# One fused hybrid layer on one core: left-over column tiles in another order, and three due times moved

## The chip, the cores and the metric

The kernel runs on one core of one Trainium2 chip. The core has five engines that run side by side, each working through its own queue in a fixed order: PE (matrix products), DVE (vector), ACT (scalar functions), POOL (a second, general elementwise engine) and SP (which here issues the DMAs). The metric is the device time of one execution in microseconds (us); lower is better.

## The reference

A layer with three branches over 2048 tokens of width 1024:

```python
h = rms_norm(x, pre_norm_g);  z = h @ w_in                      # 29 column tiles of 128
out_a = spatial_gating(u_a, v_a, ...) * silu(g_a)               # branch a
out_b = conv_module(val_b, glu_b, ...) * silu(g_b)              # branch b: 31-tap causal convolution,
                                                                # layer norm, silu, 256x256 product
out_c = rwkv7_mix(z_c, ...) * silu(g_c)                         # branch c: recurrence over tokens
mix = concat(out_a, out_b, out_c) @ w_out
x = x + rms_norm(mix, post_norm_g)
return x + (p @ ple_w) * sigmoid(x @ ple_gate_w + ple_gate_b)
```

In `rwkv7_mix` every output row also gets a bonus, `sum(r*k*r_k) * v` per head.

## The kernel before, in words

The first product, `h @ w_in`, is done in float32 as three products of a high and a low part, 48 matmuls of 128x512 per column tile and half of the tokens (line 300; two tiles at line 312 are transposed). There are two halves of 1024 tokens. In each, PE goes through the 29 column tiles in the order of the table `ORDER`; `TG[ct]` is the place of tile `ct` in it. Tiles 10 and 11 are branch b's gates, 25 to 28 those of branch c. The last six places of the second half are left over (`NT = 6`): they are not done in the column loop but, matmul by matmul, as filler among the recurrence of branch c, by the generator `tail`. Its first 45 matmuls are put ahead of the recurrence by `go(9.75)`.

All work up to the recurrence is written as generators that yield a due time in units of column tiles; `at` turns a due time into a priority, and a scheduler lays every engine's queue out from the priorities and its own time estimate of each instruction. So queues are fixed when the program is built, and an engine never overtakes an instruction that waits. From the recurrence on, PE's and DVE's orders are those of the code, but work of an earlier due time may still be laid between.

The steps that matter here:

- `s_pw` normalises the convolution's output: `parts` splits a tile into a high part (ACT, line 231) and a low part (DVE, line 232), `sums` adds over partitions on PE (line 240); mean (line 625), squares (630), square roots (637, ACT), reciprocals in four pieces (`recip`, line 245, DVE), product and silu (641, 642). Half 0 then does both gates of branch b: `pw_in` is the silu of the gate (653), `pw_out` the 256x256 product (661, PE, four matmuls a gate into two banks) and its product with the gate (664, DVE). In half 1 `tail` calls `pw_in` and `pw_out`.
- `s_prep`, last lines: the bonus of a head pair `p`: product (546), `parts`, `sums` (552, which calls line 240), product with v (553), bias (554), store (555).
- `norm_h(2)` and `norm_h(3)` load the second half's tokens. Their scale is transposed by PE (218) into two banks named `c` and copied by ACT (219). `build_h` then multiplies eight tiles by it (line 268), for one group of 512 tokens on DVE and for the other on POOL.
- `scores` (820, 825, 829) and `inverse` (861 to 886) prepare the recurrence; line 603 is branch a's spatial product.

Matmuls write to banks: the pools `m` and `c` have two each (`mps`), `z` two. The tile pool `pg` has one buffer, and every gate passes through it.

Of the kernel before, what the change touches and what calls it, by code (L numbers as in the profile page):

```python
# [34 lines left out]
def hybrid_kernel(ctx, tc, x, x_t, w_in, vecs, wup, pw_w, sgu_wt, sgu_lnb, sgu_b,  # L35
# [23 lines left out]
    def new(tag, shape=(128, 1024), dt=F32):  # L59
        return sb.tile(list(shape), dt, tag=tag, bufs=BUFS[tag], name=nm(tag))  # L60

    def at(v):

        tc.cur_priority = int(v * 1000)
# [17 lines left out]
    def mps(shape=(128, 512), tag="m"):  # L82
        return psp.tile(list(shape), F32, tag=tag, bufs=2, name=nm(tag))
# [58 lines left out]
    def col(i):  # L142
        return vc[:, i:i + 1]
# [84 lines left out]
    def parts(src, eng):  # L228

        hl = [new("mk", dt=F32R) for _ in range(2)]  # L230
        nc.scalar.copy(hl[0], src)
        eng.tensor_tensor(out=hl[1], in0=src, in1=hl[0], op=ALU.subtract)
        return hl

    def sums(ps, ones, hls, sl):

        n = 0
        for hl in hls:
            for t in hl:
                nc.tensor.matmul(ps, lhsT=ones, rhs=t[:, sl], start=(n == 0), stop=(n == 2 * len(hls) - 1))  # L240
                n += 1

    def recip(t):
        for g in range(4):
            nc.vector.reciprocal(t[:, g * 256:(g + 1) * 256], t[:, g * 256:(g + 1) * 256])  # L245
# [100 lines left out]

    ORDER = [2, 8, 3, 6, 24, 9, 7, 12, 16, 13, 20, 17, 21, 4, 14, 0, 18, 22, 15, 19, 5, 23, 1, 10, 11, 25, 26, 27, 28]
    NG = len(ORDER)  # L350
    NT = 6
    LORD = [2, 3] + [ct for ct in ORDER if ct not in (2, 3)]
    TG = {ct: i for i, ct in enumerate(ORDER)}
    W, Z, H, X = {}, {}, {}, {}
# [38 lines left out]
    def s_gemm():  # L393
        for half in range(2):
# [5 lines left out]
            while n < (NG if half == 0 else NG - NT):  # L400
                two = half == 0 and n == NG - 2
                yield b0 + n
                cts = ORDER[n:n + 2] if two else ORDER[n:n + 1]
                for ct in cts:
# [50 lines left out]
    def s_prep(half, p, st):  # L455

        b0 = half * NG
# [91 lines left out]
        for g in range(2):  # L549
            sp = mps()  # L550
            sl = slice(g * 512, (g + 1) * 512)
            sums(sp, ones64, [hl], sl)
            nc.vector.tensor_tensor(out=vs_[:, sl], in0=sp, in1=vs_[:, sl], op=ALU.mult)
        nc.scalar.activation(vs_, vs_, AF.Identity, bias=col(V_LB + p))
# [58 lines left out]
    def s_pw(half, st):  # L613

        b0 = half * NG
        t0 = half * HT
        yield b0 + NG - 8.5
        cv = [st["cv", ct] for ct in range(2)]
        hls = [parts(c, nc.vector) for c in cv]
        for g in range(2):  # L620
            sl = slice(g * 512, (g + 1) * 512)
            mp = mps()
            sums(mp, onesm, hls, sl)
            for ct in range(2):
                nc.vector.tensor_tensor(out=cv[ct][:, sl], in0=cv[ct][:, sl], in1=mp, op=ALU.subtract)
        yield b0 + NG - 7.6
        hls = []
        for ct in range(2):
            sq = new("mk")
            nc.scalar.activation(sq, cv[ct], AF.Square)  # L630
            hls.append(parts(sq, nc.vector))
        rb = new("mk")
        for g in range(2):
            sl = slice(g * 512, (g + 1) * 512)
            vp = mps()
            sums(vp, onesm, hls, sl)
            nc.scalar.activation(rb[:, sl], vp, AF.Sqrt, bias=epsr[:, 1:2])  # L637
        yield b0 + NG - 7.0
        recip(rb)
        for ct in range(2):  # L640
            nc.vector.tensor_tensor(out=cv[ct], in0=cv[ct], in1=rb, op=ALU.mult)
            nc.scalar.activation(cv[ct], cv[ct], AF.Silu, scale=col(V_CG + ct), bias=col(V_CBB + ct))
        if half == 0:
            for ct in range(2):
                yield b0 + TG[10 + ct] + 0.1
                at(b0 + TG[10 + ct] - 5)
                pw_in(half, ct, st)
                for _ in pw_out(half, ct, st):
                    pass

    def pw_in(half, ct, st):
        st["gb", ct] = gb = new("pg")
        nc.scalar.activation(gb, Z[half, 10 + ct], AF.Silu)

    def pw_out(half, ct, st):
        gb = st["gb", ct]
        for g in range(2):
            sl = slice(g * 512, (g + 1) * 512)
            pp = mps(tag="c" if half == 0 else "m")
            for k in range(2):  # L660
                nc.tensor.matmul(pp, lhsT=pw_t[:, k, ct * 128:(ct + 1) * 128], rhs=st["cv", k][:, sl],
                                 start=(k == 0), stop=(k == 1))
            yield 1.72
            nc.vector.scalar_tensor_tensor(out=gb[:, sl], in0=pp, scalar=col(V_PB + ct), in1=gb[:, sl],
                                           op0=ALU.add, op1=ALU.mult)
        nc.sync.dma_start(out=ab_s[2 + ct, :, half * HT:half * HT + HT], in_=gb)
# [3 lines left out]
    for half in range(2):  # L670
        st = {}
        S += [s_lora(half, st), s_conv(half, 0, st), s_conv(half, 1, st)]
        S += [s_prep(half, p, st) for p in range(4)]
        S += [s_sgu(half, st), s_pw(half, st)]
# [12 lines left out]
    def tail():  # L687

        cts = ORDER[NG - NT:]
        for n, ct in enumerate(cts[:-2]):  # L690
# [661 lines left out]
```

## Time and profile before

| | |
|---|---|
| time, median of 3 runs | 1438.82 us (1437.01 to 1440.38) |
| profiled execution: its time, its span | 1437.73 us, 1436.0 us |
| PE busy | 1378.8 us, 96% of the span |
| DVE, ACT, POOL busy | 1009.2, 568.6, 246.0 us |
| mean granted clock of PE | 0.987 of full speed |

The profile is of one execution. A row of a timeline gives the start and the length of a run of equal instructions on one engine, and in brackets how long the engine stood idle before it and what ended that. The granted clock of PE is given as a share of 2.4 GHz; 0.50 is 1.2 GHz. Lines in the rows are those of the kernel before. PE's columns of half 0 end at 394.5 us, and the recurrence's first scores run at 701.5.

### The profile page before, as it was taken

The numbers are of one execution on the slowest core, as the hardware profiler recorded it, in microseconds if no ns is written. First come the engines' busy times: TensorE is split into PE (matmuls) and PEld (weight loads), VectorE is DVE, ScalarE is ACT, GpSimd is POOL, SyncE is SP. The second block draws the span as 40 slices with busy tenths as digits, with TensorE's granted clock in tenths as the row PEclk, the third lists the DMA queues.
The fourth block names the chain that finished last, engine by engine and source line by source line (L and its number), as shares of the span: only waits on it lengthen the run. The fifth ranks groups of instructions, "written<-read, shape, count | busy, mean of one in ns | idle before, by whom it ended". The sixth has DMA issues, their size and how long they took to land.

```text
span 1436.0 us, 24389 instructions
## 1 busy us (share of the span) xinstructions
PE 1378.8 (96%) x9701; PEld 1102.1 (77%) x9701; DVE 1009.2 (70%) x2003; ACT 568.6 (40%) x897; POOL 246.0 (17%) x284
## 2 busy tenths in 40 slices
PE   7999999999999999999898999999998999999998
PEld 6876877887898778778676777777776777888887
DVE  6599994885537999777667588678779544545453
ACT  6334444555332343453433443544543543111121
POOL 5442221221501000000111211211221101111120
PEclk9999999999999999999899899999999999999999
DMA  8432465679534558855723833242331534242331
GB/s 335 148 147 88 150 212 181 191 277 286 208 116 153 175 175 241 231 153 192 227 89 121 291 113 95 76 140 82 109 100 56 169 124 153 99 139 99 118 117 44
DMA packets 158311, 223.29 MB, mean 155 GB/s; under 512 B 58236, under 2 KB 108149, under 8 KB 158198
## 3 DMA queue, kind: packets, MB, share of 16 engines
q1 hardware_dynamic: 158066, 221.68, 46.9%
q8 instruction: 76, 1.25, 0.4%
q14 instruction: 37, 0.30, 0.1%
q10 hardware_dynamic: 132, 0.06, 0.0%
HBM read 132.58 MB, written 89.13 MB: 154 GB/s over the span
## 4 chain that ended last, share of the span: by engine, by line
PE 73%; DVE 20%; ACT 3%; issue 2%; DMA 1%; DVEq 0%; ACTq 0%
PE z L300 33%; PE z L1164 12%; PE z L1051 8%; DVE inv L452 5%; PE c L1141 3%; PE z L312 3%; DVE inv L873 3%; PE m L820 3%; DVE inv L878 2%; PE m L240 1%; DVE mk L245 1%; DVE inv L861 1%; PE m L1120 1%; DVE L L976 1%; DMA w<-in_gate_w_dram 1%
## 5 line engine op out<-in xcount | busy, mean ns | idle before, releaser
L300 PE MATMUL z<-h,w 128*128 128x512 f32 x2592 | 630.5, 398 | 0.0
L300 PEld LDWEIGHTS z<-h,w 128*128 128x128 f32 x2592 | 484.0, 189 | 118.0 <-issue 6.4
L1051 PE MATMUL z<-h,w 128*128 128x512 f32 x768 | 206.0, 412 | 0.7 <-DVE w L1038 0.7
L452 DVE SCALAR_TENSOR_TENSOR inv<-inv,vc,inv 128x1024 f32<-128x1024 f32 x120 | 173.0, 1460 | 1.4
L1051 PEld LDWEIGHTS z<-h,w 128*128 128x128 f32 x768 | 139.9, 192 | 31.7 <-DVE w L1038 1.1
L283 POOL TENSOR_TENSOR w<-w,w 128x1024 fp32r<-128x1024 f32 x26 | 74.3, 2857 | 235.9 <-PE z L300 178.1
L1164 PE MATMUL z<-L,w 128*128 128x512 f32 (+1 forms) x384 | 96.3, 394 | 0.0
L1164 PE MATMUL z<-h,w 128*128 128x512 f32 (+1 forms) x384 | 93.1, 390 | 0.8 <-DVE inv L1147 0.8
L1148 ACT ACTIVATE inv<-inv 128x512 f32<-128x512 f32 (+1 forms) x33 | 20.4, 620 | 181.7 <-DVE inv L1147 181.7
L873 DVE TENSOR_TENSOR inv<-inv,inv 128x48 f32<-128x48 f32 (+23 forms) x464 | 85.8, 219 | 2.3
L878 DVE TENSOR_TENSOR inv<-inv,inv 128x48 f32<-128x48 f32 (+23 forms) x464 | 84.3, 217 | 1.2
L1164 PEld LDWEIGHTS z<-h,w 128*128 128x128 f32 x384 | 71.3, 188 | 17.4 <-DVE inv L1147 1.2
L1147 DVE TENSOR_TENSOR inv<-z,L 128x512 f32<-128x512 f32 (+1 forms) x32 | 21.9, 683 | 87.8 <-PE z L1164 87.8
L1164 PEld LDWEIGHTS z<-L,w 128*128 128x128 f32 x384 | 70.4, 188 | 15.3
L1108 POOL TENSOR_TENSOR inv<-inv,pg 128x1024 f32<-128x1024 f32 x16 | 38.3, 2394 | 216.9 <-DMA inv<-mx_s 117.6
L245 DVE RECIPROCAL mk<-mk 128x256 f32<-128x256 f32 x40 | 65.8, 1708 | 12.1 <-ACT mk L637 8.0
L825 DVE TENSOR_TENSOR mk<-m,mask 128x512 f32<-128x512 f32 x58 | 37.6, 685 | 35.9 <-PE m L820 31.4
L978 POOL TENSOR_TENSOR ri<-ri,pc 128x256 f32<-128x256 f32 x31 | 19.5, 630 | 236.8 <-DVE L L976 226.6
L829 ACT COPY inv<-mk 32x128 f32<-32x128 f32 x128 | 37.8, 295 | 52.9 <-DVE mk L825 50.1
L820 PE MATMUL m<-L,L 64*128 64x128 f32 x464 | 44.5, 299 | 10.1 <-DVE yn L1002 8.6
L312 PE MATMUL z<-w,h 128*128 128x256 f32 x384 | 52.6, 293 | 0.9 <-ACT h L262 0.9
L312 PEld LDWEIGHTS z<-w,h 128*128 128x128 f32 x384 | 50.3, 197 | 3.1 <-ACT h L262 1.6
(244 smaller groups left out, 1932.9 us busy)
## 6 DMA issues: line engine op xcount, KB each, us to landing
w_s<-w SPq DMA_DIRECT2D x58, 512.0 KB, 3.3
w<-w_s SPq DMA_DIRECT2D x58, 512.0 KB, 5.4
w<-in_w_in_dram SPq DMA_DIRECT2D x26, 512.0 KB, 3.5
L<-in_x_dram SPq DMA_DIRECT2D x16, 512.0 KB, 7.3
ar_s<-L SPq DMA_DIRECT2D x16, 512.0 KB, 5.0
wo_s<-w SPq DMA_DIRECT2D x16, 512.0 KB, 4.2
L<-ar_s SPq DMA_DIRECT2D x32, 256.0 KB, 3.1
L<-bk_s SPq DMA_DIRECT2D x32, 256.0 KB, 4.1
```

The lines of the kernel that those rows point to most:

```text
L245: nc.vector.reciprocal(t[:, g * 256:(g + 1) * 256], t[:, g * 256:(g + 1) * 256])
L283: nc.gpsimd.tensor_tensor(out=ws[1], in0=wr, in1=ws[0], op=ALU.subtract)
L300: nc.tensor.matmul(z[:, g * 512:(g + 1) * 512], lhsT=ws[a][:, k * 128:(k + 1) * 128], rhs=h[:, b, k, :], start=(n == 0), stop=(n == 23))
L312: nc.tensor.matmul(z[:, i * 256:(i + 1) * 256], lhsT=h[:, b, k, i * 128:(i + 1) * 128], rhs=ws[k // 4][a][:, (k % 4) * 256:(k % 4 + 1) * 2 ...
L452: nc.vector.scalar_tensor_tensor(out=ac, in0=y[:, i:i + HT], scalar=col(V_CW + 2 * i + ct), in1=ac, op0=ALU.mult, op1=ALU.add)
L820: nc.tensor.matmul(sp[par][:, p, :], lhsT=bk[lo:lo + 64, p, :], rhs=ar[lo:lo + 64, p, :], start=True, stop=True)
L873: nc.vector.tensor_tensor(out=tmp[:, o:o + n, :m], in0=tl[:, lo:hi, m:m + 1].to_broadcast([128, n, m]), in1=ml[:, m, :m].unsqueeze(1).to_b ...
L878: nc.vector.tensor_tensor(out=tl[:, lo:hi, :m], in0=tl[:, lo:hi, :m], in1=tmp[:, o:o + n, :m], op=ALU.add)
L1051: nc.tensor.matmul(mx[:, nh * 512:(nh + 1) * 512], lhsT=oT[a][:, k, :], rhs=wo[k // 4][:, b, k % 4, nh * 512:(nh + 1) * 512], start=(k == ...
L1108: nc.gpsimd.tensor_tensor(out=x2, in0=x2, in1=pg[0], op=ALU.mult)
L1141: nc.tensor.matmul(pp, lhsT=pT[:, a, k, :], rhs=gw[8 + k][b][:, nh * 512:(nh + 1) * 512], start=(n == 0), stop=(n == 5))
L1164: nc.tensor.matmul(z, lhsT=xT[a][:, k, :], rhs=gw[k][b][:, sl], start=(k == 0 and n == 0), stop=(k == 7 and n == 2))
```

## The change

Five places are edited. In `ORDER`, tiles 25 and 26 now stand ahead of 10 and 11 (places 23 and 24 instead of 25 and 26). The table serves both halves, so in half 0 the gates of branch b are the places 25 and 26 of the column loop, and in half 1 they are the third and fourth of the left-over tiles. In half 1 the three due times of the convolution's norm are 1, 1 and 0.95 tiles later. And the bonus sums of the last head pair in half 1 get the priority of 2*NG - NT + 0.1 = 52.1, behind the start of the recurrence's part at 52 (they had 51.5).

```diff
-    ORDER = [..., 5, 23, 1, 10, 11, 25, 26, 27, 28]
+    ORDER = [..., 5, 23, 1, 25, 26, 10, 11, 27, 28]
...
             sl = slice(g * 512, (g + 1) * 512)
+            if half == 1 and p == 3:
+                at(2 * NG - NT + 0.1)
             sums(sp, ones64, [hl], sl)
...
-        yield b0 + NG - 8.5
+        yield b0 + NG - (8.5 if half == 0 else 7.5)
...
-        yield b0 + NG - 7.6
+        yield b0 + NG - (7.6 if half == 0 else 6.6)
...
-        yield b0 + NG - 7.0
+        yield b0 + NG - (7.0 if half == 0 else 6.05)
```

From line 552 on, lines of the changed kernel are two higher. In the orders below a bank or buffer carries its own number, so c_2625 and c_2693 are tiles that use the two `c` banks one after the other.

PE at the end of half 0, before. Here z_2590 is tile 25, c_2441 and c_2445 are the 256x256 product for branch b's first gate (tile 10), c_2509 and c_2513 for its second (tile 11), m_2368 and m_2378 branch a's product.

```order
L661 MATMUL c_2441<-inv_699,jk_121 128x512
L661 MATMUL c_2445<-inv_699,jk_121 128x512
L300 MATMUL z_2590<-h_224,w_2347 128x512
L661 MATMUL c_2441<-inv_894,jk_121 128x512
L661 MATMUL c_2445<-inv_894,jk_121 128x512
L300 MATMUL z_2590<-h_224,w_2346 128x512 x2
L603 MATMUL m_2368<-yc_124,mk_130 64x128 x8
L603 MATMUL m_2378<-yc_124,mk_131 64x128 x3
L661 MATMUL c_2509<-inv_699,jk_121 128x512
L661 MATMUL c_2509<-inv_894,jk_121 128x512
```

The same place of the program, now: z_2574 is tile 10, z_2642 tile 11, z_2706 tile 27, w_2444 and w_2445 tile 11's weights (high and low part), c_2625 and c_2629 the first gate's product, c_2693 and c_2697 the second's.

```order
L300 MATMUL z_2574<-h_289,w_2347 128x512
L663 MATMUL c_2625<-inv_699,jk_121 128x512
L663 MATMUL c_2625<-inv_894,jk_121 128x512
L663 MATMUL c_2629<-inv_699,jk_121 128x512
L663 MATMUL c_2629<-inv_894,jk_121 128x512
L300 MATMUL z_2642<-h_224,w_2444 128x512 x2
L663 MATMUL c_2693<-inv_699,jk_121 128x512
L663 MATMUL c_2693<-inv_894,jk_121 128x512
L663 MATMUL c_2697<-inv_699,jk_121 128x512
L663 MATMUL c_2697<-inv_894,jk_121 128x512
L300 MATMUL z_2706<-h_224,w_2504 128x512 x2
L300 MATMUL z_2642<-h_224,w_2445 128x512
```

Behind the bonus sums of half 0's last pair stood 11 column matmuls (L300), then the first product; now 57 column matmuls, branch a's product and the transposes of line 218 stand between. The two gates' products are now two column matmuls apart.

DVE at the end of half 0, before: the products with the gates (pg), branch a's (mk_2367), the copies for the transposed scale (L215) and the eight multiplications of the next half's tokens (L268).

```order
L664 SCALAR_TENSOR_TENSOR pg_2439<-c_2441,vc,pg_2439 128x512
L664 SCALAR_TENSOR_TENSOR pg_2439<-c_2445,vc,pg_2439 128x512
L607 SCALAR_TENSOR_TENSOR mk_2367<-m_2368,vc,yn_125 128x512
L215 COPY mk_2542<-rs_2539 128x512
L215 COPY mk_2574<-rs_2571 128x512
L607 SCALAR_TENSOR_TENSOR mk_2367<-m_2378,vc,yn_125 128x512
L610 TENSOR_TENSOR mk_2367<-mk_2367,mk_2136 128x1024
L664 SCALAR_TENSOR_TENSOR pg_2507<-c_2509,vc,pg_2507 128x512
L664 SCALAR_TENSOR_TENSOR pg_2507<-c_2513,vc,pg_2507 128x512
L268 TENSOR_TENSOR L_2550<-L_2550,mk_2542 128x512 x2
```

And now, from the first of the eight on:

```order
L268 TENSOR_TENSOR L_2534<-L_2534,mk_2526 128x512 x2
L268 TENSOR_TENSOR L_2536<-L_2536,mk_2526 128x512 x2
L268 TENSOR_TENSOR L_2538<-L_2538,mk_2526 128x512 x2
L268 TENSOR_TENSOR L_2540<-L_2540,mk_2526 128x512 x2
L666 SCALAR_TENSOR_TENSOR pg_2623<-c_2625,vc,pg_2623 128x512
L666 SCALAR_TENSOR_TENSOR pg_2623<-c_2629,vc,pg_2623 128x512
L666 SCALAR_TENSOR_TENSOR pg_2691<-c_2693,vc,pg_2691 128x512
L666 SCALAR_TENSOR_TENSOR pg_2691<-c_2697,vc,pg_2691 128x512
```

All four products with the gates, which are what reads the `c` banks, went from ahead of the eight multiplications to behind them.

DVE ahead of the recurrence, before: reciprocals of the norm (mk_4740), the low part for the bonus sums (mk_4849), the norm's products (L641), the bonus products (L553, which read the banks m_4852 and m_4856), branch a's.

```order
L245 RECIPROCAL mk_4740<-mk_4740 128x256 x4
L232 TENSOR_TENSOR mk_4849<-L_4473,mk_4848 128x1024
L641 TENSOR_TENSOR inv_3223<-inv_3223,mk_4740 128x1024
L641 TENSOR_TENSOR inv_3421<-inv_3421,mk_4740 128x1024
L553 TENSOR_TENSOR L_4724<-m_4852,L_4724 128x512
L553 TENSOR_TENSOR L_4724<-m_4856,L_4724 128x512
L607 SCALAR_TENSOR_TENSOR mk_4862<-m_4863,vc,yn_125 128x512
```

And now:

```order
L245 RECIPROCAL mk_4826<-mk_4826 128x256 x2
L232 TENSOR_TENSOR mk_4841<-L_4473,mk_4840 128x1024
L245 RECIPROCAL mk_4826<-mk_4826 128x256 x2
L555 TENSOR_TENSOR L_4702<-m_4844,L_4702 128x512
L555 TENSOR_TENSOR L_4702<-m_4848,L_4702 128x512
L643 TENSOR_TENSOR inv_3223<-inv_3223,mk_4826 128x1024
L643 TENSOR_TENSOR inv_3421<-inv_3421,mk_4826 128x1024
L609 SCALAR_TENSOR_TENSOR mk_4854<-m_4855,vc,yn_125 128x512
```

The low part now stands between the two halves of the reciprocals, and the bonus products ahead of the norm's. On PE the four bonus sums follow, now as before, on all eight sums of squares, but those end later:

```order
L300 MATMUL z_4922<-h_2839,w_4649 128x512
L240 MATMUL m_4827<-mk_4817,onesm 128x512
L240 MATMUL m_4833<-mk_4817,onesm 128x512
L240 MATMUL m_4827<-mk_4822,onesm 128x512
L240 MATMUL m_4833<-mk_4822,onesm 128x512
L240 MATMUL m_4827<-mk_4823,onesm 128x512
L240 MATMUL m_4833<-mk_4823,onesm 128x512
L240 MATMUL m_4844<-mk_4840,ones_83 128x512
L240 MATMUL m_4848<-mk_4840,ones_83 128x512
L240 MATMUL m_4844<-mk_4841,ones_83 128x512
L240 MATMUL m_4848<-mk_4841,ones_83 128x512
L605 MATMUL m_4855<-yc_124,mk_133 64x128 x8
```

Before, the last sums of squares (m_4741, m_4747) had 11 column matmuls of the first left-over tile (z_4922) and eight transposes between themselves and the bonus sums; now those stand ahead of the last sums of squares.

## Rows read from the trace of the kernel before

**Rows 1.** The page: busy time of all engines, and the chain that ended last by engine.

```profile
PE 1378.8 (96%) x9701; PEld 1102.1 (77%) x9701; DVE 1009.2 (70%) x2003; ACT 568.6 (40%) x897; POOL 246.0 (17%) x284
...
PE 73%; DVE 20%; ACT 3%; issue 2%; DMA 1%; DVEq 0%; ACTq 0%
```

**Rows 2.** What PE itself waited for over the whole span: engine, tile, line, the engine and line waited for, us in total, times, longest.

```profile
PE m L240 <- ACT mk L231: 5.5, 3, 3.4
...
PE m L240 <- DVE mk L232: 3.5, 2, 2.6
...
PE m L603 <- DVE L L553: 1.6, 1, 1.6
```

**Rows 3.** Timeline of PE at the end of half 0: start, length, line, what, how many.

```profile
337.05 2.73 PE L300 MATMUL z<-h,w 128*128 128x512 f32 x11
...
345.30 1.99 PE L661 MATMUL c<-inv,jk 128*128 128x512 f32 x4
347.21 0.65 PE L603 MATMUL m<-yc,mk 128*64 128x128 f32 x6
...
350.07 12.59 PE L300 MATMUL z<-h,w 128*128 128x512 f32 x53
362.50 1.04 PE L218 MATMUL c<-ident,mk 128*128 128x128 f32 x8
363.29 31.39 PE L300 MATMUL z<-h,w 128*128 128x512 f32 x134
394.52 11.68 PE L312 MATMUL z<-w,h 128*128 128x256 f32 x96
```

**Rows 4.** The chain that ended last, in order of time: start, length; branch a's product where nothing is laid between it.

```profile
603.20 1.90 PE m L603 x32
```

**Rows 5.** Timeline of DVE at the end of half 0.

```profile
342.63 1.61 DVE L664 SCALAR_TENSOR_TENSOR pg<-c,vc,pg 128x512 f32<-128x512 f32 x2 [0.27 <-PE c L661]
...
363.76 13.08 DVE L268 TENSOR_TENSOR L<-L,mk 128x512 f32<-128x512 f32 x8 [7.14 <-ACT mk L219]
```

**Rows 6.** Timeline of POOL there.

```profile
361.99 2.39 POOL L283 TENSOR_TENSOR w<-w,w 128x1024 fp32r<-128x1024 f32 x1 [9.32 <-ACT w L282]
364.33 13.65 POOL L268 TENSOR_TENSOR L<-L,mk 128x512 f32<-128x512 f32 x8
```

**Rows 7.** Timeline of DVE later, while POOL is idle: one multiplication of two tiles in SBUF, of the size of line 268's.

```profile
665.37 0.69 DVE L517 TENSOR_TENSOR L<-L,L 128x512 f32<-128x512 f32 x1
```

**Rows 8.** PE after a gap of 3.38 us, and stretches of 3 us around it: start and end, length, busy (matmuls), granted clock, DMA share, GB/s.

```profile
141.34 1.22 PE L240 MATMUL m<-mk,ones 128*128 128x512 f32 x2 [3.38 <-ACT mk L231]
...
138.00:141.00 3.00, 0.00 (x0) 0.93 0.00 0
141.00:144.00 3.00, 2.66 (x5) 0.50 0.00 0
144.00:147.00 3.00, 3.00 (x8) 0.50 0.00 0
147.00:150.00 3.00, 3.00 (x13) 0.93 0.53 175
```

**Rows 9.** Timeline of PE ahead of the recurrence.

```profile
686.20 0.61 PE L240 MATMUL m<-mk,onesm 128*128 128x512 f32 x2
...
689.22 1.03 PE L537 MATMUL m<-ident,L 128*128 128x128 f32 x8
691.43 0.98 PE L240 MATMUL m<-mk,ones 128*128 128x512 f32 x2 [1.18 <-ACT mk L231]
695.07 1.22 PE L240 MATMUL m<-mk,ones 128*128 128x512 f32 x2 [2.65 <-DVE mk L232]
697.93 3.68 PE L603 MATMUL m<-yc,mk 128*64 128x128 f32 x32 [1.64 <-DVE L L553]
701.54 0.58 PE L820 MATMUL m<-L,L 64*128 64x128 f32 x1
...
728.69 1.98 PE L661 MATMUL m<-inv,jk 128*128 128x512 f32 x4 [0.67 <-ACT L L839]
```

**Rows 10.** PE in stretches of 1.5 us there (columns as in rows 8).

```profile
693.00:694.50 1.50, 0.00 (x0) 0.68 0.87 285
...
702.00:703.50 1.50, 1.50 (x16) 0.50 0.24 96
703.50:705.00 1.50, 1.50 (x6) 0.91 0.03 8
```

**Rows 11.** Timelines of DVE and ACT there.

```profile
687.35 6.59 DVE L245 RECIPROCAL mk<-mk 128x256 f32<-128x256 f32 x4 [6.14 <-ACT mk L637]
693.85 1.16 DVE L232 TENSOR_TENSOR mk<-L,mk 128x1024 fp32r<-128x1024 f32 x1
694.93 2.35 DVE L641 TENSOR_TENSOR inv<-inv,mk 128x1024 f32<-128x1024 f32 x2
697.19 1.28 DVE L553 TENSOR_TENSOR L<-m,L 128x512 f32<-128x512 f32 x2
...
730.71 0.75 DVE L664 SCALAR_TENSOR_TENSOR pg<-m,vc,pg 128x512 f32<-128x512 f32 x1 [1.12 <-PE m L661]
...
686.62 1.27 ACT L637 ACTIVATE mk<-m,epsr 128x512 f32<-128x512 f32 x2 [9.08 <-PE m L240]
690.33 1.05 ACT L231 CAST mk<-L 128x1024 fp32r<-128x1024 f32 x1
```

More of the change, by code (lines that the diff above doesn't have):

```diff
@@ L345, in split @@
         nc.vector.tensor_tensor(out=dst_lo, in0=src, in1=dst_hi, op=ALU.subtract)
-    ORDER = [2, 8, 3, 6, 24, 9, 7, 12, 16, 13, 20, 17, 21, 4, 14, 0, 18, 22, 15, 19, 5, 23, 1, 10, 11, 25, 26, 27, 28]
+    ORDER = [2, 8, 3, 6, 24, 9, 7, 12, 16, 13, 20, 17, 21, 4, 14, 0, 18, 22, 15, 19, 5, 23, 1, 25, 26, 10, 11, 27, 28]
     NG = len(ORDER)
```

## The prediction

> **What bounds the kernel now.** I read the page's busy shares and its chain first, then what PE waited for, then PE's timeline where the two orders of instructions differ. PE is busy 96% of the span and carries 73% of the chain [rows 1], so a change that moves work without adding any can move the end only by making or removing time in which PE stands, or runs at the low one of its two clock levels. The list of PE's waits is short; the part that this change aims at is the wait for the sums of line 240 and for branch a's product [rows 2]. On the timeline these are the gaps of 1.18, 2.65 and 1.64 us between 690.2 and 697.9 [rows 9], 5.47 us together. The clock makes them dearer: it falls during them and reads 0.50 until shortly after 703.5 [rows 10]. PE never stands between 337 and 394 us, where each run of matmuls begins when the one before ends [rows 3].
>
> PE's order is the same in both kernels up to the last bonus sums of half 0, then differs until the end of half 0's columns, and again from the convolution's norm in half 1 on. I work out both places against the profiled execution, whose own time, 1437.73 us, is 1.09 under the median shown.
>
> **The end of half 0: a new wait.** The four products with the gates on DVE (line 664) now stand behind the eight multiplications of line 268. They free the two c banks, and PE's product for the second gate needs both again, two column matmuls after the first gate's. So I time both sides.
>
> PE: from 337.05 on it has, up to the second gate's product, 57 + 2 column matmuls, branch a's product, eight transposes and the first gate's product. A column matmul takes (362.50 - 350.07)/53 = 0.2345 us, branch a's product 1.90 [rows 4], the transposes 363.29 - 362.50 = 0.79, two L661 rows (four records) 347.21 - 345.30 = 1.91 [rows 3], and there are two such pairs; the second overlaps the column matmuls behind it, so 3.4 to 3.8 for both. That is 337.05 + 13.8 + 1.9 + 0.8 + 3.6 = 357.2.
>
> DVE: 41 of the column matmuls and branch a's product come before the transposes, which so begin at 337.05 + 9.6 + 1.9 = 348.6. Before, the multiplications began 1.26 us after the transposes did (363.76 against 362.50 [rows 3, 5]), so now at 349.8. They take 13.08 us for eight [rows 5], since POOL does the other group's eight at the same time in 13.65 [rows 6]: 1.64 each, against 0.69 for a like multiplication with POOL idle [rows 7]. In the new order the pair still begins together, as both wait for ACT's copies of the same transposes. So they end at 362.9, and the first product with a gate, half of 1.61 [rows 5], at 363.7.
>
> The row shows a multiplication of two SBUF tiles stretched to 2.4 times its length beside POOL. The Trainium skill, SBUF — State Buffer, section "Who interferes with whom", says that a DVE instruction with two SBUF inputs and a GpSimd instruction that reads SBUF take turns at one shared port, the second blocked for the whole of the first; by that the eight and eight alternate, which these rows bear out (13.08 and 13.65 for both together), and nothing about the change lets them run side by side. It is the rule that speaks against the change: without it the eight would end at 349.8 + 8 x 0.69 = 355.3, ahead of PE.
>
> PE therefore stands from 357.2 to 363.7, 6.5 us. What is behind: everything, since nothing on PE's queue can pass the product. After this gap the clock has to be paid too. The nearest row is the gap of 3.38 us at 141: the clock falls during it, reads 0.50 from 141 to 147 and 0.93 in the three us after [rows 8], so PE ran 6.1 us at half its level and lost 3.0. A gap twice as long will hardly cost less: I take 3.0, with 0 (no fall) and 3.4 (half of the 6.8 us between fall and rise) as ends. From 394 to the norm of half 1 nothing gives it back: PE's run has no slack there, and the end of half 0 hides only waits that are shorter than it. Sum here: +9.5 us.
>
> Other instructions moved past here are covered. The low part of tile 11's weights, on POOL, is now behind POOL's eight: 349.8 + 0.6 (by which POOL began behind DVE) + 13.65 + 2.39 = 366.4 [rows 5, 6], and PE needs it at 363.7 + 3.4 + 0.5 = 367.6; the cover is 1.2 us, and what goes beyond would be added. SP's store of the second gate waits for tile 11, 367.6 + 46 x 0.2345 + 3.0 = 381.4 by this account, and loads of half 1's weights stand behind it; they are wanted at 394.5 + 9.5 = 404, some 20 us later.
>
> **Ahead of the recurrence: the gaps are moved, not removed.** Up to the first scores PE has the same matmuls as before, so I compare when they begin; the shift of 9.5 us is left out. The last sums of squares now come after the transposes. All else done, they are issued at 690.25 - 0.45 = 689.8 (690.25 is where the gap of 1.18 begins [rows 9]). Before, ACT's square root began 0.42 after that issue (686.62 against 686.20 [rows 9, 11]): now 690.2. Its first half ends at 690.85, the cast for the bonus sums (1.05) at 691.9: PE stands 1.7. DVE began its reciprocals 0.73 after the first square root [rows 11]: now 690.95. Two of four end 3.3 later, at 694.25; the low part (1.16) at 695.4: PE stands 3 more. Then two reciprocals (698.6), and the first of the two bonus products (0.64), which frees the bank for branch a's product: 699.25, where it was 697.93. The norm's products (2.35) now come behind the bonus products, ahead of what reads branch a's bank: 699.9 + 2.3 + 0.7 = 702.9 for the first scores; PE itself is ready at 699.25 + 3.68 = 702.9. Before: 701.54. So +1.4, with the same low clock.
>
> Behind that, the gap of 0.67 at 728.69 (a product for a gate that waited for a bank [rows 9]) goes, as the products now stand elsewhere: -0.7. In their new places DVE may wait for PE inside the inverse, as it did for 1.12 us [rows 11]; then the inverse ends later, and the recurrence with it: 0 to 1.5, of which I take 0.3. The fourth gate's product sits in the recurrence, two column matmuls behind scores whose banks it needs; DVE needs 0.69 to free one: 0 to 0.5. Sum: +1.0, ends -1 and +4 (a further fall of the clock).
>
> **The rivals.** (a) Forecast: both as worked out, 9.5 + 1.0 = +10.5, that is 1448.2 against the profiled 1437.73, and 1449.3 against the median. (b) No wait at the end of half 0, because the eight run at 0.69 or start earlier; only the +1.0 is left, 1439.8. For it speaks only that the scheduler laid it out so; against it, rows 5 and 6. (c) The wait at half 0 is there, but the new places do clear the gaps ahead of the recurrence: 5.47 and some 3 of clock go, 1438.8 + 9.5 - 8.5 = 1439.8, no change to speak of. Against it: the chain of ACT and DVE between sums of squares and branch a's product is as long as before, and starts later. (d) Faster: the gaps ahead of the recurrence go and half 0 has no wait, 1438.8 - 8.5 = 1430. It decides if the eight take under 0.9 us each, and if the bonus sums get their parts while column matmuls are left; the order shows none left. (e) More: the clock falls a second time at the inverse or the waits of the recurrence shift, 1453 to 1456.
>
> The low level at rows 8 is 1.2 GHz, and PE stood for 3.38 us before it fell. The Trainium skill, TensorE: Matmul & The Clock Gate, Part 1, says that activity lifts the gate and idling brings it back, and that only these two levels exist, which rows 8 and 10 bear out (0.50 and 1.00, mixed values only where a stretch holds both); no run here shows whether a gap of 6.5 us costs more than one of 3.38.
>
> **How the numbers follow.** (a) 0.77, (b) 0.05, (c) 0.06, (d) 0.04, (e) 0.08. The predicted time is that of (a), 1449.3. Its ends: gap 5.5 to 7.2 (the ends of PE's 3.4 to 3.8 and half a us for where POOL and DVE start), clock 0 to 3.4, ahead of the recurrence -1 to +4: rarely all at one end, so 1443 to 1454. With (e) half in, 1442 to 1455; left out are (b), (c), (d) and the rest of (e), some 0.18. A measurement of this kernel can tell about 0.2%, 2.9 us, from no change: slower are (a) and (e), 0.85; same (b) and (c), 0.11; faster (d), 0.04.
>
> **What would show it.** A row of PE at line 663 near 363 with 6 to 7 us idle before it, ended by DVE; the granted clock at 0.50 for about 6 us behind it; DVE's eight at 13 us from 349.8 on; half 1's first matmul of line 312 at about 404. Ahead of the recurrence, counted from the first idle: gaps at the first bonus sum, at its low part and at branch a's product, 6 to 8 us together, and the first scores 1 to 2 us later than the shift alone makes them. I am wrong if line 663 begins without idle there, or if branch a's product near 707 has no gap ahead of it.

## The result, and the profile after

The changed kernel takes 1450.05 us (median of 4 runs, 1447.46 to 1452.09) against 1438.73 for the kernel before: the ratio is 1.0075, with a 95% interval of 1.0056 to 1.0095, so it is slower, by 11.3 us between the medians. The profiled execution took 1448.92 us, its span is 1447.2. PE's busy time, in which a matmul at the low clock counts with its longer length, is unchanged (1378.6 us, 1378.8 before), so the 11.2 us by which the span grew are time in which PE stood. Lines from 552 on are two higher than in the rows of before.

The list of PE's waits, of which these are five lines (us in total, times, longest), has a new entry, for the second gate's product of half 0, and the three waits ahead of the recurrence [rows 2] are still there:

```profile
PE m L822 <- DVE yn L1004: 9.5, 5, 1.9
PE c L663 <- DVE pg L666: 5.8, 1, 5.8
PE m L240 <- ACT mk L231: 5.1, 3, 2.7
PE m L240 <- DVE mk L232: 3.3, 2, 2.5
PE m L605 <- DVE L L555: 2.6, 1, 2.6
```

PE's timeline at the end of half 0, the counterpart of [rows 3]:

```profile
349.45 1.03 PE L218 MATMUL c<-ident,mk 128*128 128x128 f32 x8
354.04 3.60 PE L663 MATMUL c<-inv,jk 128*128 128x512 f32 x8
357.07 1.03 PE L300 MATMUL z<-h,w 128*128 128x512 f32 x2
363.88 5.20 PE L663 MATMUL c<-inv,jk 128*128 128x512 f32 x8 [5.78 <-DVE pg L666]
...
401.92 1.35 PE L312 MATMUL z<-w,h 128*128 128x256 f32 x10
```

DVE and then POOL there (compare [rows 5, 6]). DVE's eight multiplications end at 363.17, and the first product with a gate, which frees a bank, only behind them:

```profile
350.71 12.46 DVE L268 TENSOR_TENSOR L<-L,mk 128x512 f32<-128x512 f32 x8 [3.20 <-ACT mk L219]
363.09 1.40 DVE L666 SCALAR_TENSOR_TENSOR pg<-c,vc,pg 128x512 f32<-128x512 f32 x2
...
351.24 13.05 POOL L268 TENSOR_TENSOR L<-L,mk 128x512 f32<-128x512 f32 x8 [14.37 <-DMA w<-in_w_in_dram]
364.26 4.64 POOL L283 TENSOR_TENSOR w<-w,w 128x1024 fp32r<-128x1024 f32 x2
```

Busy time by windows around the gap (length of the window, then busy time and instructions of PE, its weight loads, DVE, ACT and POOL; the third number from the end is the granted clock): in this execution it falls 2 us after PE stopped, and most of the low stretch passes while PE still stands. Here the row at 1.00 shows the high one of the two levels; rows 8 and 10, from which the prediction quotes 1.00, hold no such stretch.

```profile
358.00:360.00 2.00, 0.10 (x1) 0.00 (x0) 2.00 (x3) 0.00 (x0) 2.00 (x2) 1.00 0.78 305
360.00:362.00 2.00, 0.00 (x0) 0.00 (x0) 2.00 (x2) 1.04 (x1) 2.00 (x2) 0.52 0.00 0
362.00:364.00 2.00, 0.12 (x1) 0.12 (x1) 2.00 (x3) 0.00 (x0) 2.00 (x2) 0.50 0.00 0
364.00:366.00 2.00, 2.00 (x3) 0.97 (x4) 0.48 (x1) 0.00 (x0) 2.00 (x2) 0.50 0.33 131
366.00:368.00 2.00, 2.00 (x4) 0.81 (x4) 0.00 (x0) 0.00 (x0) 2.00 (x2) 0.77 1.01 406
```

PE ahead of the recurrence, the counterpart of [rows 9]: the gaps are 1.48, 2.46 and 2.59 us instead of 1.18, 2.65 and 1.64.

```profile
696.30 1.57 PE L240 MATMUL m<-mk,onesm 128*128 128x512 f32 x6
699.35 1.09 PE L240 MATMUL m<-mk,ones 128*128 128x512 f32 x2 [1.48 <-ACT mk L231]
702.89 1.22 PE L240 MATMUL m<-mk,ones 128*128 128x512 f32 x2 [2.46 <-DVE mk L232]
706.70 3.68 PE L605 MATMUL m<-yc,mk 128*64 128x128 f32 x32 [2.59 <-DVE L L555]
710.31 0.58 PE L822 MATMUL m<-L,L 64*128 64x128 f32 x1
```

DVE there, against [rows 11]: the low part between the halves of the reciprocals, the bonus products last.

```profile
698.39 3.36 DVE L245 RECIPROCAL mk<-mk 128x256 f32<-128x256 f32 x2 [1.53 <-ACT mk L639]
701.67 1.16 DVE L232 TENSOR_TENSOR mk<-L,mk 128x1024 fp32r<-128x1024 f32 x1
702.75 3.35 DVE L245 RECIPROCAL mk<-mk 128x256 f32<-128x256 f32 x2
706.02 1.22 DVE L555 TENSOR_TENSOR L<-m,L 128x512 f32<-128x512 f32 x2
```

How far the changed kernel is behind, at places of the same work (start before, start after):

| place | before | after | behind by |
|---|---|---|---|
| first column matmul behind half 0's last bonus sums (L300) | 337.05 | 337.82 | 0.77 |
| half 1's first matmul (L312) | 394.52 | 401.92 | 7.40 |
| first scores | 701.54 | 710.31 | 8.77 |
| tenth step of the recurrence (L943, now L945) | 877.51 | 885.30 | 7.79 |
| twentieth step | 1008.57 | 1017.11 | 8.54 |
| end of the span | 1436.0 | 1447.2 | 11.2 |

So in this pair of profiles 6.6 us come from the end of half 0 and 1.4 from the work ahead of the scores, of which 1.0 is won back in the inverse, where the wait of 0.67 is gone; 3.4 come from the recurrence and what follows it, and 0.8 were there before the orders part.

### The profile page after: what moved, and what is told of

Read it like the earlier page. It is cut to its first block, busy times and chain, and to the rows that moved or that the text cites. A ratio compares the mean times of both kernels' runs of the same rounds, so it can differ in the third digit from the quotient of the medians.

```text
span 1447.2 us, 24393 instructions
## 1 busy us (share of the span) xinstructions
PE 1378.6 (95%) x9701; PEld 1100.8 (76%) x9701; DVE 1007.4 (70%) x2003; ACT 568.8 (39%) x897; POOL 241.9 (17%) x284
## 4 chain that ended last, share of the span: by engine, by line
PE 71%; DVE 22%; ACT 3%; issue 2%; DMA 1%; DVEq 0%; ACTq 0%
PE z L300 30%; PE z L1166 12%; PE z L1053 8%; DVE inv L452 6%; PE c L1143 3%; DVE inv L875 3%; PE z L312 3%; PE m L822 3%; DVE inv L880 2%; PE m L240 1%; DVE mk L245 1%; DVE inv L863 1%; PE m L1122 1%; DVE L L978 1%; PE c L945 1%
## 5 line engine op out<-in xcount | busy, mean ns | idle before, releaser
L300 PE MATMUL z<-h,w 128*128 128x512 f32 x2592 | 631.0, 398 | 1.5 <-ACT zl L336 1.4
L300 PEld LDWEIGHTS z<-h,w 128*128 128x128 f32 x2592 | 483.7, 189 | 119.6 <-issue 6.4
L283 POOL TENSOR_TENSOR w<-w,w 128x1024 fp32r<-128x1024 f32 x26 | 70.4, 2710 | 227.0 <-PE z L300 183.9
L312 PE MATMUL z<-w,h 128*128 128x256 f32 x384 | 52.1, 291 | 0.9 <-ACT h L262 0.9
L312 PEld LDWEIGHTS z<-w,h 128*128 128x128 f32 x384 | 49.9, 196 | 3.1 <-ACT h L262 1.6
```

Of the source, the lines that this page charges most:

```text
L283: nc.gpsimd.tensor_tensor(out=ws[1], in0=wr, in1=ws[0], op=ALU.subtract)
L300: nc.tensor.matmul(z[:, g * 512:(g + 1) * 512], lhsT=ws[a][:, k * 128:(k + 1) * 128], rhs=h[:, b, k, :], start=(n == 0), stop=(n == 23))
L312: nc.tensor.matmul(z[:, i * 256:(i + 1) * 256], lhsT=h[:, b, k, i * 128:(i + 1) * 128], rhs=ws[k // 4][a][:, (k % 4) * 256:(k % 4 + 1) * 2 ...
```

## Experiments

All ratios are to the kernel before, run on the same chip between the others; each kernel ran 5 to 12 times. The median of before was 1439.8 to 1440.2 us there, and "above before" is counted from it. A ratio is not the quotient of the two medians, so the two can differ by a few hundredths of a per cent.

| kernel | median us | ratio (95% interval) |
|---|---|---|
| half 1's edits only | 1444.92 | 1.0034 (1.0021 to 1.0048) |
| half 0's new order only | 1449.74 | 1.0076 (1.0047 to 1.0105) |
| change, second gate in other banks | 1442.32 | 1.0018 (1.0005 to 1.0031) |
| change, DVE multiplies both groups | 1442.82 | 1.0028 (1.0012 to 1.0045) |
| change, DVE six and POOL ten | 1447.64 | 1.0055 (1.0039 to 1.0071) |
| change without the rank | 1450.70 | 1.0064 (1.0049 to 1.0079) |
| gates third and fourth in half 1 only | 1442.05 | 1.0015 (1.0002 to 1.0028) |
| later norm in half 1 only | 1444.24 | 1.0029 (1.0015 to 1.0044) |
| before, bonus sums pulled ahead | 1442.59 | 1.0013 (1.0000 to 1.0026) |
| the same, and gates third and fourth in half 1 | 1436.33 | 0.9970 (0.9961 to 0.9979) |
| the same, and the later norm | 1441.53 | 1.0014 (1.0001 to 1.0027) |

**The two halves apart.** One kernel keeps the old places in half 0, the other has the new ones in half 0 alone:

```diff
+    ORD = (ORDER[:23] + [10, 11, 25, 26, 27, 28], ORDER)
...
-                cts = ORDER[n:n + 2] if two else ORDER[n:n + 1]
+                cts = ORD[half][n:n + 2] if two else ORD[half][n:n + 1]
```

> The changed kernel, but half 0 goes through its column tiles in the old order (gates of branch b at places 23 and 24); half 1 is as changed. Theory: of the 11 us, 6 to 7 come from the wait for the two c banks at the end of half 0, and the rest (about 4.5) from half 1's edits, part of it ahead of the first scores, part in the recurrence. Then PE has no idle row at the second gate's product of half 0, line 312 of half 1 begins near 394.5, and the time is 1443 (1441.5 to 1444.5). Rival 1: all that is lasting comes from half 0, and what half 1 shows is chance: 1438.7 plus or minus 1. Rival 2: the wait at half 0 is made good later, and half 1's edits cost it all: 1449 to 1450.

> The kernel before, but half 0 goes through its column tiles in the new order; half 1 with its left-over tiles, due times and bonus sums is as before. Theory: the wait of about 5.8 us at the second gate's product and some 1.5 us of clock behind it are all that is added: 1438.7 + 6.6 to 7.3 = 1445.3 to 1446.0, first scores 6.6 to 7.4 later than before. Rival 1 (all from half 0): 1449 to 1450. Rival 2 (all from half 1): 1438.7. If the two parts add up, this one's surplus and that of the run with half 1's edits alone make the 11.3 us together.

With the old half 0, half 1's edits alone measured 5.1 us above before, a little more than the theory's 4.3; PE runs straight through the place of the gap:

```profile
353.75 9.70 PE L300 MATMUL z<-h,w 128*128 128x512 f32 x41
```

With half 0's order alone the wait is back, the same to a hundredth:

```profile
365.22 5.22 PE L663 MATMUL c<-inv,jk 128*128 128x512 f32 x8 [5.79 <-DVE pg L666]
```

Both halves therefore cost. It is the first kernel that puts out both rivals: its interval, 3.0 to 6.9 us above before, holds neither nothing nor the whole 11.3. The second alone would not, for its median lies in the range of rival 1: it was 9.9 us above before, not 6.6 to 7.3, and the two surpluses make 15.0 us together, not 11.3. Its six executions fall into two lots: 1445.17 to 1446.09 at a mean granted clock of 0.986 to 0.988, like before's (5.4 to 6.3 above before's median, near the theory; with these the two surpluses make 10.5 to 11.4), and 1453.39 to 1456.84 at 0.978 to 0.981. That the lower lot is the one to add up was not said beforehand. The profiled one, 1453.39, is of the second lot; its clock was 0.95 from 1100 to 1200, where PE's order is that of before and before's clock is 0.98:

```profile
1100.00:1200.00 100.00, 90.94 (x927) 71.69 (x924) 60.35 (x182) 41.87 (x75) 6.08 (x7) 0.95 0.37 118
```

**Is it the bank, and is it DVE beside POOL?** Three kernels take the wait apart. The first gives the second gate's product other banks, the second lets DVE multiply both groups of tokens, the third moves two of DVE's eight multiplications to POOL:

```diff
-            pp = mps(tag="c" if half == 0 else "m")
+            pp = mps(tag="c" if half == 0 and ct == 0 else "m")
...
-        X[g] = (xt, rb[:, 1], nc.vector if g % 2 == 0 else nc.gpsimd)
+        X[g] = (xt, rb[:, 1], nc.vector if g != 1 else nc.gpsimd)
...
-            eng.tensor_tensor(out=xt[k], in0=xt[k], in1=rb, op=ALU.mult)
+            (nc.gpsimd if t > 10 and k >= 6 else eng).tensor_tensor(out=xt[k], in0=xt[k], in1=rb, op=ALU.mult)
```

> The changed kernel, but the second gate's product of half 0 writes to the two m banks, the first still to c. The scheduler then issues it ahead of the transposes; DVE's four products with the gates still stand behind its eight multiplications. Theory (the wait is for banks that DVE frees late): no idle row at this product, no low clock near 361 to 367, line 312 of half 1 near 394.5 to 396, and 1443 to 1444 as with half 0 in the old order. Rival: PE wants a bank of DVE's there in any case (the m banks for the next user, or the buffer pg for the next silu), so the wait turns up at another row of half 0 with 5 us or more, and the time stays at 1448 to 1450.

> The changed kernel, but in half 1 DVE multiplies both groups of tokens (sixteen instructions of line 268 in a row), POOL none; the second gate's product of half 0 is then issued some 35 column matmuls later. Theory (a multiplication takes 1.6 us only because POOL does the other group's beside it): each takes 0.7, the sixteen 11.2, from 349.8 to 361; the product finds its banks free and PE has no idle row there; 1443 to 1444. Rival (it takes 1.6 us here whoever works beside it, because of its place or what else goes on): the sixteen take 26, to 376, and PE stands some 10 us at the product: 1452 or more.

> The changed kernel, but in half 1 DVE multiplies six of its eight tiles in line 268 and POOL ten instead of eight; PE's order is untouched. By 1.56 us a multiplication (12.46 for eight) DVE is done 3.1 us earlier, so PE's idle time at the second gate's product of half 0 should be 2.7 instead of 5.78 us. The question is the clock. Theory 1 (the clock falls some 2 us after PE stops and the low level then lasts as long whatever PE does, so that a shorter gap leaves more of it to be run through): low from about 360 to 367 as before, 3.0 us lost instead of 1.5, so only 1.5 us are gained up to line 312 of half 1 and the time is 1448.5. Theory 2 (a gap of 2.7 is short enough for no fall): 3.1 + 1.5 = 4.6 gained, 1445.4. A wait of up to 2 us for the low part of tile 11's weights, which is two multiplications later on POOL, would take that much from either.

With other banks no product with a gate in half 0 waits any more, although DVE's products still stand behind its eight (the first at 367.74); by the ratios it is 0.57%, 8.2 us, below the changed kernel, where the trace gives 7.3 for the gap and the clock behind it. With DVE alone, sixteen multiplications take less than eight did beside POOL. That is 0.74 us each against 1.56, and POOL was not idle throughout: one of the sixteen, beside a multiplication of POOL's in line 283, took 2.9 us. The last ten, the second row here, took 0.61 each:

```profile
352.02 11.90 DVE L268 TENSOR_TENSOR L<-L,mk 128x512 f32<-128x512 f32 x16 [3.20 <-ACT mk L219]
357.82 6.10 DVE L268 TENSOR_TENSOR L<-L,mk 128x512 f32<-128x512 f32 x10
```

There the second gate's product stands later too (367.39) and has no wait; this kernel does not show what the faster multiplications would give with PE's order unchanged. The third kernel leaves PE's order alone. Its gap is 2.43 us, as worked out, and the low part of tile 11's weights, later on POOL, now costs 1.92:

```profile
362.06 5.29 PE L663 MATMUL c<-inv,jk 128*128 128x512 f32 x8 [2.43 <-DVE pg L666]
369.73 1.66 PE L300 MATMUL z<-h,w 128*128 128x512 f32 x6 [1.92 <-POOL w L283]
```

Its clock fell all the same, 2.2 us into the gap, so theory 2 does not hold in this execution. Theory 1 is only half right: PE was back earlier, but the clock was back earlier too:

```profile
360.00:362.00 2.00, 0.00 (x0) 0.00 (x0) 2.00 (x3) 0.55 (x1) 2.00 (x2) 0.97 0.23 92
362.00:364.00 2.00, 1.94 (x3) 0.91 (x4) 0.66 (x2) 0.49 (x1) 2.00 (x3) 0.50 0.24 96
364.00:366.00 2.00, 2.00 (x5) 0.90 (x4) 0.00 (x0) 0.00 (x0) 2.00 (x2) 0.68 1.01 408
```

That is half of 1.94 and 0.32 of 2.00 us, 1.6 lost, against half of 2.12 and 0.23 of 2.00, 1.5, after the gap of 5.78. The kernel's 1447.64 is 2.4 below the changed kernel's 1450.05 (2.9 by the ratios, whose intervals overlap); 3.35 less gap and 1.92 more wait make 1.4. One profile cannot choose between the two theories of the clock: what the same gap costs differs from execution to execution, as the kernel without the rank shows below.

**Half 1's edits apart.**

```diff
-    ORDER = [..., 5, 23, 1, 10, 11, 25, 26, 27, 28]
+    ORDER = [..., 5, 23, 1, 25, 26, 10, 11, 27, 28]
+    ORD = (ORDER[:23] + [10, 11, 25, 26, 27, 28], ORDER)
...
-        yield b0 + NG - 8.5
+        yield b0 + NG - (8.5 if half == 0 else 7.5)
...
-            if half == 1 and p == 3:
-                at(2 * NG - NT + 0.1)
```

The first kernel has only the gates' new places in half 1, the second only the three later due times, the third the whole change but the rank.

> Of the change only the gates of branch b as third and fourth of the left-over tiles; half 0, the norm's due times and the bonus sums as before. Theory: up to the first scores everything is as before (gaps of 5.47 us together); behind them the wait of 0.67 for a gate's bank goes, and ACT has three square roots of the recurrence behind two copies that it had ahead of them before, 0.45 us each (the waits of 1.89 instead of 1.44 us). Sum +0.7: 0.05% slower than before (1439.5 to 1442). Rival (the gates in their new places are what half 1's edits cost): 1443 to 1445, as with the later norm added.

> Of the change only the later due times of half 1's norm; column tiles of both halves and the bonus sums as before. Theory: the sums of squares and with them the reciprocals come about 3 us later, the waits ahead of branch a's product grow from 5.5 to 6.5 us and the first scores are 1.4 us later; one square root behind the copies, 0.45: +1.9, 1441 to 1443. Rival (the later norm is harmless, the gates cost): 1440 or less.

> The changed kernel without the line that ranks the last pair's bonus sums behind. The program built from it has the same instructions in the same order on all five engines as the changed kernel, so every theory expects the changed kernel's time: 0.75% above the kernel before, plus or minus 0.2, with the gap of 5.8 us at the second gate's product and the gaps of 1.5, 2.5 and 2.6 ahead of the first scores. It also shows how far executions of one and the same program lie apart in the recurrence, by their mean clock.

The rank does nothing: without its two lines every engine's order is word for word that of the changed kernel, and so is the time within the intervals. That makes its profile a second one of the changed kernel's program, and there the clock behind the same gap at half 0 costs twice as much:

```profile
363.04 6.74 PE L661 MATMUL c<-inv,jk 128*128 128x512 f32 x8 [5.77 <-DVE pg L664]
...
360.00:362.00 2.00, 0.00 (x0) 0.00 (x0) 2.00 (x2) 1.03 (x1) 2.00 (x3) 1.00 0.00 0
362.00:364.00 2.00, 0.96 (x1) 0.50 (x2) 1.64 (x3) 0.00 (x0) 2.00 (x2) 0.59 0.00 0
364.00:366.00 2.00, 2.00 (x4) 0.91 (x3) 0.00 (x0) 0.00 (x0) 2.00 (x2) 0.50 0.76 307
366.00:368.00 2.00, 2.00 (x3) 0.77 (x3) 0.00 (x0) 0.00 (x0) 2.00 (x1) 0.50 1.03 403
368.00:370.00 2.00, 2.00 (x5) 0.88 (x4) 0.00 (x0) 0.00 (x0) 0.04 (x1) 0.71 0.90 264
```

PE stopped at 357.27, and the clock was at 1.00 until 362.3, 5 us into the gap; so PE was back for nearly all of the low stretch. That is half of 0.96 and of twice 2.00, and 0.29 of 2.00 us: 3.1 lost where the changed kernel's profile has 1.5, and half 1's first matmul is 8.1 us behind before's instead of 7.4.

The later norm is what moves the gaps. Alone, it gives the three waits of the changed kernel to a hundredth:

```profile
692.76 1.08 PE L240 MATMUL m<-mk,ones 128*128 128x512 f32 x2 [1.48 <-ACT mk L231]
696.30 1.22 PE L240 MATMUL m<-mk,ones 128*128 128x512 f32 x2 [2.46 <-DVE mk L232]
700.11 1.12 PE L603 MATMUL m<-yc,mk 128*64 128x128 f32 x8 [2.59 <-DVE L L553]
```

and with the gates alone they are before's 1.18, 2.65 and 1.64. The medians, 2.2 above before for the gates and 4.4 for the norm, are 1.5 and 2.5 above what was expected; the first interval (0.3 to 4.0) holds the expectation, the second (2.2 to 6.3) begins just above it, and its median lies outside the range given (1441 to 1443).

**Can the gaps be cleared?** ACT's cast for the bonus sums stood at 690.33 behind the square roots [rows 11], while ACT was idle for 9 us before those: the cast waited not for its rank but for a free buffer of the pool `mk`, for in a program built with an earlier rank alone it keeps its place in ACT's order, and in one with tiles of another pool it stands ahead of the square roots. So three kernels pull the bonus sums ahead instead. The first is before with these edits; the second also has the gates third and fourth in half 1 alone; the third the later norm too.

```diff
-        hl = parts(rs_, nc.vector)
+        hl = parts(rs_, nc.vector, "w" if half == 1 and p == 3 else "mk")
...
-            sp = mps()
+            sp = mps(tag="c" if half == 1 and p == 3 else "m")
...
+        if half == 1 and p == 3:
+            at(b0 + TG[20 + p] - 5)
```

> The kernel before, with the last pair's bonus sums pulled ahead instead of ranked behind: their high and low part go to two tiles of the pool w instead of mk, their sums to the banks c instead of m, and their priority is that of the pair's own columns. ACT's cast then stands ahead of the square roots, DVE's low part ahead of the reciprocals, and PE's four sums lie among column matmuls. Theory (the 5.47 us of idle time ahead of the first scores are the wait for these parts, and these parts waited for a buffer): the gaps of 1.18 and 2.65 are gone, the first scores run near 695.2, when DVE has done the two products behind its reciprocals, against 701.5; the third gate's product then waits some 2.6 us for the norm's silu, which ends near 700.3. Sum -3.7, 1436, and down to 1432 if the clock does not fall. Rival (the gaps only move, as in the changed kernel: reciprocals and norm are as late as ever and PE stands for them): 1438 to 1440.

> The same bonus sums pulled ahead, and of the change only the gates of branch b as third and fourth of the left-over tiles (half 0 in the old order, due times of the norm as before, no rank of 52.1). Theory: first scores near 696 (5.5 us earlier), the wait of the gates' products for the norm's silu is gone since they stand some 20 us later; a wait of about 1 us for the first masked scores, as DVE does the norm's products ahead of them. Sum -5 to -6 and part of the 5.1 us of clock lost there: 1433 (1430 to 1436). Rival (the gates in their new places cost by themselves, in the inverse or in the recurrence): 1438 or more, no better than the bonus sums alone.

> As the run before it in this list, but with the change's later due times of half 1's norm too. Theory: the sums of squares are the last before branch a's product, so the reciprocals on DVE run from about 690.5 to 697.5 and hold up the products that free the banks for the first scores: PE stands 3 to 4 us between branch a's product and the scores, and the clock falls as before. First scores near 699, 1436 to 1438, 2 to 4 us more than with the due times as before. Rival (with the bonus sums out of the way the later norm costs nothing, or helps): equal to the other run or less, 1433 or below.

The second is the version that beats both kernels: 1436.33 us, 0.30% below before (0.21 to 0.39%), all of its 12 executions at 1438.04 or less. PE and DVE there; one gap of 3.52 us is left, for the reciprocals:

```profile
692.20 1.97 PE L607 MATMUL m<-yc,mk 128*64 128x128 f32 x32 [0.28 <-ACT mk L541]
697.69 0.54 PE L824 MATMUL m<-L,L 64*128 64x128 f32 x1 [3.52 <-DVE mk L611]
...
680.23 1.21 DVE L232 TENSOR_TENSOR w<-L,w 128x1024 fp32r<-128x1024 f32 x1
689.25 6.59 DVE L245 RECIPROCAL mk<-mk 128x256 f32<-128x256 f32 x4 [6.67 <-ACT mk L641]
695.75 1.22 DVE L557 TENSOR_TENSOR L<-c,L 128x512 f32<-128x512 f32 x2
696.89 1.40 DVE L611 SCALAR_TENSOR_TENSOR mk<-m,vc,yn 128x512 f32<-128x512 f32 x2
```

The gain, 3.9 us between the medians, is smaller than the 5 to 6 expected: DVE idles until 689.25 and takes the two bonus products, whose sums were there at 687.6, only behind the reciprocals. With the gates in their old places nothing is gained: 1442.59, a miss for theory and rival alike. Its first scores ran 2.1 us earlier than before's (at 699.42, with the same wait of 3.52), the third gate's product did not wait, and it was 1.2 us ahead until the fifteenth step of the recurrence; what it lost came behind that. With the later norm the wait for the same instruction is 5.2 us:

```profile
PE m L824 <- DVE mk L611: 5.2, 1, 5.2
```

and the kernel takes 5.2 us more than the second, more than the 2 to 4 expected. The rival that the gates cost by themselves holds only where the bonus sums are late (2.2 us, 0.3 to 4.0, see above): with the bonus sums ahead they are worth 6 us. Only 1.0 of these has a cause that the traces show: three square roots of ACT's, see below, stand late in the first of the three kernels and not in the second, and PE's waits for them make 9.5 and 8.5 us. Another part is the clock, on average 0.9865 over the executions of the first and 0.9882 over those of the second; if PE had been busy throughout that would be 2.4 us (an estimate). Why it differs, and the rest, is open.

## Why the prediction was right, point by point

The time, 1449.3, was 0.8 below the median. That it came so close is in part luck: the end of half 0, forecast 9.5, took 6.6 in the changed kernel's profile (8.2 in the other one of the same program), and the recurrence, forecast at nothing, took 3.4.

- **The gap at half 0**, forecast 6.5: 5.78. The place, the releaser and the two sides were as worked out: PE done at 358.1 (forecast 357.2), DVE's eight from 350.7 (349.8) for 12.46 (13.08). The kernel with other banks shows that the bank is the cause.
- **The multiplication's price**, 1.64 against 0.69: measured 1.56 beside POOL, and 0.61 with POOL idle, for the same instruction at the same place. POOL's own took 1.23 with DVE done (four in 4.93, behind 362.43, in the kernel with six and ten), and in turns the two would take 1.84 a pair; together they took 1.70 (eight pairs from 350.71 to 364.29). The Trainium skill, SBUF — State Buffer, section "Who interferes with whom", says that such a pair takes turns at one shared port; these runs bear that out to 0.15 us a pair, and not only a row.
- **The clock behind the gap**, forecast 3.0: 1.5 in the changed kernel's profile, 3.1 in that of the kernel without the rank, which is the same program. The step that does not hold is the reason, "a gap twice as long will hardly cost less": the price is not set by the length of the gap. What differs between the two profiles is when the clock fell, 2 or 5 us into the gap, and with it how much of the stretch at 0.50 was spent standing. The gap at 141 shows the same: the clock fell 2.6 us into it (the prediction says after 3.38), and PE was back 0.8 us later [rows 8]. At that place PE has a gap in every profile; where it is 2.7 us long, it cost 3.1 to 3.4 us in seven profiles, 1.7 in two (half 1's edits only, and the gates alone) and nothing in two (other banks, and the later norm with the bonus sums ahead). So 3.0 was one draw of several; the ends given, 0 and 3.4, hold them all.
- **The sum at half 0**: with the gap this makes 7.3, of which 6.6 show between 337 and half 1's first matmul. The new order itself takes PE some 0.8 us less there: in the two kernels with this order and no wait (other banks, DVE alone) that stretch is 0.9 and 0.8 us shorter than before's. The forecast left that out.
- **The cover of 1.2 us for tile 11's weights** held: no wait in the changed kernel. With two more multiplications on POOL it was used up, and 1.92 us appeared.
- **Ahead of the recurrence**, forecast +1.4 at the scores: 8.77 - 7.40 = 1.4, with gaps at the three places named, 6.5 us together (forecast 6 to 8). By the single runs it is the later norm that makes them.
- **The inverse and the gates**, forecast -0.7 + 0.3: -1.0 (8.77 to 7.79), so of the 0.3 for DVE's waits nothing shows there.
- **The recurrence**, forecast nothing: 3.4. A part of it is an order that the forecast did not look at. At the steps where ACT has the square root of the output's norm behind two copies, PE waits 1.89 us for it, where it is ahead of them 1.44. The changed kernel has two square roots more behind the copies, so 0.9. ACT before and after, at the same step:

```profile
996.60 0.30 ACT L999 ACTIVATE grs<-grs,epsr 128x8 f32<-128x8 f32 x1 [0.86 <-DVE grs L998]
996.81 0.35 ACT L952 COPY L<-c 64x256 f32<-64x256 f32 x1
997.18 0.37 ACT L953 COPY L<-c 64x256 f32<-64x256 f32 x1
...
1004.42 0.37 ACT L954 COPY L<-c 64x256 f32<-64x256 f32 x1 [0.59 <-PE c L951]
1004.81 0.37 ACT L955 COPY L<-c 64x256 f32<-64x256 f32 x1
1005.20 0.30 ACT L1001 ACTIVATE grs<-grs,epsr 128x8 f32<-128x8 f32 x1
```

The kernel with half 0's order alone has them late too, so no edit of half 1 is needed for it; presumably it comes with the scheduler's own time estimates. It was not tried by itself.

Of the other 2.5 us, 1.5 come where the clock falls near 1060, which it does in the changed kernel's profile alone. Before's falls near 1110 instead, and that costs it little, since PE has no wait for ACT's copies in the step after it, where the changed kernel stands 1.54 us (at 1126.90). Behind the scores the two lose about as much by the clock, 9.3 us before and 8.8 after. The last 1.0 is spread over smaller waits. In the other profile of the changed program the clock falls at yet other places, and between the scores and the end it loses 0.8 us instead of 2.4.

Beyond the single profiles half 1's edits came out at 2.5 to 5.1 us above before in the three kernels that have them and no wait at half 0, where the trace of the one with half 1's edits only shows 0.5 up to the recurrence's sixth step (1.3 behind there less the 0.8 at half 1's first matmul) and 0.9 at the waits for square roots behind it. A part of the rest goes with the clock: on average over the executions it was 0.985 in the kernel with half 1's edits only and in that with the later norm only, 0.986 with the gates only, and 0.987 in before beside them. So more was lost by the clock with the edits, and not in the profiled executions alone; why is open.

Of the rivals, (b) to (d) are refuted by the wait itself and by the gaps. (e) was wrong in its place, the inverse, and its price (1453 to 1456) was not reached, but waits of the recurrence did shift.

## What to carry to other kernels

A table that two loops share is changed in both: here the larger part of the loss came from the half that had no gap to clear. When work is moved behind an in-order engine's long block, ask what that block's late result frees (here the banks that matmuls write to), and change the bank before changing the place. And when a small step is late, look at what its output buffer waits for before ranking it: the rank moved nothing, while another pool for two tiles and other banks, with the gates moved in one half, made the kernel 0.3% faster than before.

## What the runs showed of the hardware

- The price of the clock follows neither from the length of a gap nor from the program: a gap of 5.8 us cost 1.5 and 3.1 us at the low level in two profiles of the same order of instructions, one of 2.43 us cost 1.6, and one of 2.7 us near 142 between nothing and 3.4 in eleven profiles.
- Executions of one program differ by as much as the change under study: the kernel with half 0's order alone ran from 1445.17 to 1456.84 us, with mean granted clocks of 0.988 and 0.978. At that spread a median over a handful of executions may move by several us, and terms of 1 us have to be read from where the two timelines part.
- A DVE multiplication of two SBUF tiles takes 0.61 us with POOL idle and 1.56 with POOL doing the same, so the pair of engines did sixteen in 13.6 us (350.71 to 364.29) and DVE alone in 11.9.
